# Expert weights read as two neighbouring rows to a partition, in a two-layer diffusion block on one core

## The chip, the cores and the metric

The kernel runs on one core of a Trainium2 chip. The metric is device time in microseconds of one execution, lower is better. All arithmetic on the chip is in 32-bit floats; the large projections split each operand into a high and a low part and take three products.

## The reference, cut to what matters

256 latent tokens and 256 context tokens of width 1024 go through two layers. A layer has four token mixers (a gated delta rule and three attentions), a gated merge of their outputs, an output projection with a first layer norm, and an expert-choice feed-forward with a second norm. The change is about the feed-forward and what feeds it:

```python
def expert_choice_ffn(h, w_router, w_gate, w_up, w_down):
    aff = jax.nn.softmax(jnp.einsum('bnd,de->bne', h, w_router), axis=-1)
    gval, idx = lax.top_k(jnp.swapaxes(aff, 1, 2), cap)        # cap = 32 tokens for each of 16 experts
    xg = jax.vmap(lambda hb, ib: hb[ib])(h, idx)
    a = jnp.einsum('becd,edf->becf', xg, w_gate)
    u = jnp.einsum('becd,edf->becf', xg, w_up)
    y = jnp.einsum('becf,efd->becd', jax.nn.silu(a) * u, w_down)
    ...
```

Each expert has three 1024 x 1024 weight matrices, 12 MB of float32. With 16 experts and two layers that is 384 MB, read once. A sum over d or f may be taken in any order, as long as the rows of the weights and the entries of the tokens are paired alike.

## The kernel before, in words

Work is written in program order and a scheduler of the language orders it on each engine; waits are semaphores. All weight loads are issued by SyncE (SP), one after another in one queue: an SP instruction that waits holds back all loads behind it.

**Streams of weights.** `wload` (L123) loads 1 MB into a tile "w" of 128 partitions x 2048 numbers. `split` and `hilo` (L130, L145) cut a projection's weights into a high part "wh" (copied by ACT) and a low part "wl" (subtracted by DVE or POOL); each part is a tile of 128 x 1024 of its own, three buffers deep (`parts`, L141).

**Merge** (`merge`, L1128). For each of the four branches, in the order 0, 3, 2, 1, the branch's transposed output is loaded from DRAM into "oT" (written oTm), split into "oh" (ACT) and "ol" (DVE), each with one buffer, and multiplied by the branch's weights, split into "bh" and "bl": 8 groups of 6 products (ps_br). Between these groups stand the products of the gates (ps_gate, 24 to a group). Gates of some branches were computed before and come back from DRAM as "thm".

**Output projection, router, experts.** `out_project` (L1164) ends with the first norm and `route`, which transposes the rows of the residual "xz" (ps_xT, L1284) for the router. `moe` then gathers the chosen tokens with one-hot products (ps_xg, L1413; "xgT" holds the result, the contraction on the partitions), four experts at a time, and works through 16 experts: 4 pieces of w_gate_e, 4 of w_up_e (ps_gu, L1458), a transposition of the activated values "eac" (ps_aT, L1475), 4 pieces of w_down_e (ps_dn, L1489). A piece is 256 rows of a weight matrix, 1 MB. `wl` (L1324) gives each piece a slot in turn: 1 MB tiles "w", or pairs of 512 KB tiles "we" that other stages have left (wh with wl, bh with bl, oT with oh), 13 slots in layer 0. Partition p of a piece holds row p and row p + 128: two runs of 4 KB. A pair of tiles takes two DMAs.

```python
# L1327
rows = src[l, e, kk * 256:(kk + 1) * 256, :].rearrange("(k p) f -> p k f", p=P)
# L1340, a pair of tiles
for k, (pool, tag, n) in enumerate(slot):
    w = pool.tile([P, 1024], F32, tag=tag, name="we", bufs=n)
    nc.sync.dma_start(w, rows[:, k])
```

**Modulation** (`mod`, L220): the six vectors of each token stream that scale and shift the norms are a product with w_mod; its pieces are loaded as [128, 2048], 8 KB to a partition. At the start every second piece goes through two tiles "wm" of 512 KB.

## Time and profile before

| | |
|---|---|
| median of 3 runs | 2174.92 us (2173.11, 2174.92, 2190.13) |
| span of the profiled execution | 2171.3 us |
| bytes moved by DMA in it | 553.92 MB |
| busy: PE, DVE, ACT, POOL | 1849.2, 955.9, 503.8, 350.6 us |
| experts of layer 0, first gathered product to last weight | about 729 to 1219 us |
| experts of layer 1 | about 1702 to 2151 us |

The profile is of one execution, and its time is its span; nothing else of that execution is on record. It lies 3.6 us under the median. PE is TensorE's products, PEld its loads of the stationary operand (beside PE). A queue's share is the time that its packets took, over 16 DMA engines and the stretch; packets overlap a little, so it can pass 100%. "A <- B" in a list of waits means that A sat idle until B was done.

### The profile page before, as it was taken

The page shows a single profiled execution, that of the slowest core. Times are in us where ns is not written, and L with a number is a line of the kernel's source. Part 1 is how long each engine was busy: PE and PEld are TensorE (multiplying, and loading weights), DVE is VectorE, ACT ScalarE, POOL GpSimd, SP SyncE. Part 2 cuts the span into 40 slices and gives each one's busy share as a digit, 9 for nine tenths or more (in the row PEclk, how much of TensorE's full clock was granted, in tenths as well). Part 3 has the DMA queues.
Part 4 walks back from the last instruction along what each step waited for, and adds up shares of the span by engine and source line. Part 5 has one row for each costly group of instructions (what it writes and reads, how often), then busy time and mean ns, then how long its engine had stood idle before and what let it go on. Part 6 is the DMA issues. An engine that isn't in the chain of part 4 may idle for free. (4 is left out here: it accounts for less than half of the span.)

```text
span 2171.3 us, 33547 instructions
## 1 busy us (share of the span) xinstructions
PE 1849.2 (85%) x13730; PEld 1199.7 (55%) x13730; DVE 955.9 (44%) x2126; ACT 503.8 (23%) x1038; POOL 350.6 (16%) x380
## 2 busy tenths in 40 slices
PE   6898899989999899988797898899899886676665
PEld 2676778867788555322222376778889542232221
DVE  3859547773226424221121486977755430110102
ACT  2332116752222111000000332246543100000000
POOL 1151330012532000000000125330264000000000
PEclk9999999998999899999999999999999896777767
DMA  7445413117333589999999655302487899999996
GB/s 290 161 170 194 156 36 108 54 59 260 110 126 137 211 335 350 409 409 409 409 409 409 239 194 182 130 24 96 134 271 265 323 408 409 409 409 409 409 409 274
DMA packets 200181, 553.92 MB, mean 255 GB/s; under 512 B 16222, under 2 KB 83164, under 8 KB 194396
## 3 DMA queue, kind: packets, MB, share of 16 engines
q1 hardware_dynamic: 190960, 538.56, 65.6%
q10 hardware_dynamic: 9068, 13.23, 1.7%
q8 instruction: 108, 1.77, 0.3%
q14 instruction: 45, 0.37, 0.1%
HBM read 541.25 MB, written 10.49 MB: 254 GB/s over the span
## 5 line engine op out<-in xcount | busy, mean ns | idle before, releaser
L1458 PE MATMUL ps_gu<-w,xgT 128*32 128x256 f32 (+1 forms) x1632 | 241.2, 533 | 69.5 <-DMA w<-in_w_gate_e_dram 35.5
L149 POOL TENSOR_TENSOR wl<-w,wh 128x1024 fp32r<-128x1024 f32 x62 | 154.1, 2486 | 884.1 <-DMA w<-in_w_in_dram 504.2
L1458 PE MATMUL ps_gu<-we,xgT 128*32 128x256 f32 (+1 forms) x1440 | 204.1, 512 | 38.8 <-DMA we<-in_w_up_e_dram 24.3
L1458 PEld LDWEIGHTS ps_gu<-w,xgT 128*32 128x32 f32 (+1 forms) x1632 | 78.8, 134 | 212.1 <-issue 83.0
L1500 DVE TENSOR_TENSOR y<-ps_dn,g2r 32x512 f32<-32x512 f32 (+1 forms) x128 | 70.9, 554 | 259.0 <-PE ps_dn L1489 257.5
L311 PE MATMUL ps_gate<-hh,wh 128*128 128x512 f32 (+1 forms) x512 | 179.8, 351 | 0.4 <-ACT wh L148 0.4
L313 PE MATMUL ps_gate<-hh,wl 128*128 128x512 f32 (+1 forms) x512 | 179.5, 351 | 0.0
L312 PE MATMUL ps_gate<-hl,wh 128*128 128x512 f32 (+1 forms) x512 | 179.4, 350 | 0.0
L148 ACT CAST wh<-w 128x1024 fp32r<-128x1024 f32 x124 | 129.6, 1049 | 179.2 <-PE ps_gate L312 77.3
L1458 PEld LDWEIGHTS ps_gu<-we,xgT 128*32 128x32 f32 (+1 forms) x1440 | 63.1, 128 | 167.3 <-DMA we<-in_w_up_e_dram 62.1
L1489 PE MATMUL ps_dn<-w,eaT 128*32 128x256 f32 (+1 forms) x896 | 119.1, 522 | 32.5 <-DMA w<-in_w_down_e_dram 26.8
L1468 ACT ACTIVATE eth<-ps_gu 128x512 f32<-128x512 f32 (+1 forms) x32 | 15.7, 491 | 518.4 <-PE ps_gu L1458 518.4
L311 PE MATMUL ps_n<-wh,hh 128*128 128x256 f32 x400 | 116.7, 292 | 7.3 <-DVE c_v L861 3.1
L312 PE MATMUL ps_n<-wl,hh 128*128 128x256 f32 x400 | 115.8, 290 | 8.2 <-POOL wl L149 8.2
L1471 DVE SCALAR_TENSOR_TENSOR eac<-eth,ps_gu 128x512 f32<-128x512 f32 (+1 forms) x32 | 17.7, 554 | 235.1 <-PE ps_gu L1458 235.1
L149 DVE TENSOR_TENSOR wl<-w,wh 128x1024 fp32r<-128x1024 f32 x62 | 85.9, 1385 | 72.9 <-ACT wh L148 72.6
L313 PE MATMUL ps_n<-wh,hl 128*128 128x256 f32 x400 | 115.9, 290 | 0.0
L1489 PE MATMUL ps_dn<-we,eaT 128*32 128x256 f32 (+1 forms) x640 | 93.4, 512 | 15.6 <-DMA we<-in_w_down_e_dram 11.1
L311 PEld LDWEIGHTS ps_gate<-hh,wh 128*128 128x128 f32 x512 | 99.4, 194 | 11.4 <-ACT wh L148 0.8
L312 PEld LDWEIGHTS ps_gate<-hl,wh 128*128 128x128 f32 x512 | 99.2, 194 | 10.8
L313 PEld LDWEIGHTS ps_gate<-hh,wl 128*128 128x128 f32 x512 | 99.0, 193 | 10.8 <-DVE wl L149 0.2
L1470 DVE SCALAR_TENSOR_TENSOR eth<-eth,ps_gu 128x512 f32<-128x512 f32 (+1 forms) x32 | 17.7, 554 | 193.3 <-ACT eth L1468 193.3
(453 smaller groups left out, 3591.2 us busy)
## 6 DMA issues: line engine op xcount, KB each, us to landing
w<-in_w_gate_e_dram SPq DMA_DIRECT2D x75, 1024.0 KB, 13.2
w<-in_w_down_e_dram SPq DMA_DIRECT2D x72, 1024.0 KB, 12.7
w<-in_w_up_e_dram SPq DMA_DIRECT2D x62, 1024.0 KB, 13.9
we<-in_w_up_e_dram SPq DMA_DIRECT2D x120, 512.0 KB, 13.4
w<-in_w_in_dram SPq DMA_DIRECT2D x54, 1024.0 KB, 5.2
we<-in_w_down_e_dram SPq DMA_DIRECT2D x108, 512.0 KB, 14.0
we<-in_w_gate_e_dram SPq DMA_DIRECT2D x96, 512.0 KB, 13.9
w<-in_w_mod_dram SPq DMA_DIRECT2D x44, 1024.0 KB, 5.0
```

The lines of the kernel that those rows point to most:

```text
L148: nc.scalar.copy(h, w)
L149: (nc.gpsimd if j else nc.vector).tensor_tensor(x, w, h.bitcast(F32), op=OP.subtract)
L311: nc.tensor.matmul(ps, lh[k], rh[k], start=(k == 0), stop=False)
L312: nc.tensor.matmul(ps, lh[k], rl[k], start=False, stop=False)
L313: nc.tensor.matmul(ps, ll[k], rh[k], start=False, stop=(k == nk - 1))
L1458: nc.tensor.matmul(ps[M * q:M * q + M, :NF], xg[e // 4][:, 2 * kk + k, e % 4, :], w[k][:, q * NF:(q + 1) * NF], start=(kk == 0 and k == 0) ...
L1468: nc.scalar.activation(th, pss[0][:, :NF], AF.Tanh, scale=0.5)
L1470: nc.vector.scalar_tensor_tensor(th, th, 1.0, pss[0][:, :NF], op0=OP.add, op1=OP.mult)
L1471: nc.vector.scalar_tensor_tensor(ac, th, 0.5, pss[1][:, :NF], op0=OP.mult, op1=OP.mult)
L1489: nc.tensor.matmul(py[M * q:M * q + M, :NF], av[:, fc % nj, fc // nj, :], w[k][:, q * NF:(q + 1) * NF], start=(fc == 0), stop=(fc == 7))
L1500: nc.vector.tensor_tensor(ys[w][32 * e4:32 * e4 + 32, q * NF:(q + 1) * NF], py[o:o + 32, :NF], g2r[o:o + 32, q * NF:(q + 1) * NF], op=OP.mult)
```

## The change

A piece of an expert's weights still has 256 rows, but partition p now holds the rows 2p and 2p + 1, which lie side by side in DRAM: one run of 8 KB. The two halves of a piece are then the even and the odd rows, so everything that is contracted with them is put in the same order by reading with a step of two numbers (`pairs`): the residual's rows in the gather and in the router's transpositions, the activated values in theirs, the router's weights, and the columns of gain, bias and modulation that are applied to the gathered tokens. For these columns the modulation's vectors 3 and 4 are transposed a second time into "modp", and their biases and the first norm's gain and bias are loaded a second time into "vecp", in runs of two numbers.

The pairs of 512 KB tiles become single tiles: wh and wl are the halves of "whl", bh and bl those of "bhl", oT and oh those of "oth". A slot is then filled by one DMA. In layer 0, one early slot (ol with y1) stays a pair, as do two in layer 1. Some small tiles share buffers between the layers.

```diff
 def parts(self, n):
-        return [self.whs[self.nwh].tile([P, 1024], F32R, tag=g, name=g)[:, :n] for g in ("wh", "wl")]
+        t = self.whs[self.nwh].tile([P, 2, 1024], F32R, tag="whl", name="whl")
+        return [t[:, i, :n] for i in range(2)]
 def mod(self, l, g):
-                w = []
-                for j, tag in enumerate(("wh", "wl")):
-                    w.append(self.whp.tile([P, 1024], F32, tag=tag, name="wm"))
-                    nc.sync.dma_start(w[j], src[:, j * 1024:(j + 1) * 1024])
+                w = self.whp.tile([P, 2, 1024], F32, tag="whl", name="wm")
+                nc.sync.dma_start(w.rearrange("p a b -> p (a b)"), src)
+                w = [w[:, 0], w[:, 1]]
...
+        if g:
+            pt = self.pt.tile([P, 512], F32, tag="t", name="ps_mp")
+            for a in range(2):
+                for j in range(2):
+                    nc.tensor.transpose(pt[:, (2 * a + j) * P:(2 * a + j + 1) * P], self.pairs(rows)[:, a, j], self.c("ident"))
...
+            for w2 in range(2):
+                nc.vector.tensor_tensor(dst[:, :, :, w2], src[:, :, :, w2], bc, op=OP.add)
 def merge(self, l, br, first):
-        oT = self.mg.tile([P, 2, 512], F32, tag="oT", name="oTm", bufs=1)
+        oth = self.mg.tile([P, 2, 2, 512], F32R, tag="oth", name="oth", bufs=1)
+        oT, oh = oth[:, 0].bitcast(F32), oth[:, 1]
         nc.sync.dma_start(oT[:, :, :n], self.oT[br])
         ol = self.mg.tile([P, 2, 512], F32R, tag="ol", name="ol", bufs=1)
-        oh = self.mg.tile([P, 2, 512], F32R, tag="oh", name="oh", bufs=1)
...
-                bh, bl = (self.mg.tile([P, 2, 512], F32R, tag=x, name=x, bufs=2) for x in ("bh", "bl"))
+                bhl = self.mg.tile([P, 2, 2, 512], F32R, tag="bhl", name="bhl", bufs=2)
+                bh, bl = bhl[:, 0], bhl[:, 1]
+def pairs(x):
+        return x.rearrange("p (a q j) -> p a j q", q=P, j=2)
 def route(self, t, stats):
-                nc.tensor.transpose(ps[j][:, k * P:(k + 1) * P], z[:, kc * P:(kc + 1) * P], self.c("ident"))
+                nc.tensor.transpose(ps[j][:, k * P:(k + 1) * P], self.pairs(z)[:, kc // 2, kc % 2], self.c("ident"))
 def moe(self, l):
-            order = [self.wpb] * self.NW2[l] + [[(mg, "bh", 2), (mg, "bl", 2)]] * 2 + [[(mg, "oT", 1), (mg, "oh", 1)]]
+            order = [self.wpb] * self.NW2[l] + [[(mg, "bhl", 2)]] * 2 + [[(mg, "oth", 1)]]
...
-                rows = src[l, e, kk * 256:(kk + 1) * 256, :].rearrange("(k p) f -> p k f", p=P)
+                rows = src[l, e, kk * 256:(kk + 1) * 256, :].rearrange("(p k) f -> p k f", k=2)
+                flat = src[l, e, kk * 256:(kk + 1) * 256, :].rearrange("(p k) f -> p (k f)", k=2)
...
-                                nc.tensor.matmul(po, self.xz[:, off[w] + i, k * P:(k + 1) * P],
+                                nc.tensor.matmul(po, self.pairs(self.xz[:, off[w] + i])[:, k // 2, k % 2],
...
-                    nc.tensor.transpose(ps[:, j * P:(j + 1) * P], ac[:, j * P:(j + 1) * P], self.c("ident"))
+                    nc.tensor.transpose(ps[:, j * P:(j + 1) * P], self.pairs(ac)[:, j // 2, j % 2], self.c("ident"))
 def run(self):
+                for i, r in enumerate((R_BMOD + 24, R_L1G)):
+                    nc.scalar.dma_start(self.vecp[:, 16 * i:16 * i + 16].rearrange("p (v j) -> p v j", j=2),
+                                        a["vecs"][l, r:r + 16, :].rearrange("r c -> (r c)").rearrange("(v q j) -> q v j", q=P, j=2))
```

On SP, the loads of layer 0's first two experts stood like this before ("w" and "we" are slots, the last number of a row how often it is repeated):

```order
L127 DMA w<-in_w_down_e_dram 128x2x1024
L1343 DMA we<-in_w_down_e_dram 128x1024 x6
L127 DMA w<-in_w_gate_e_dram 128x2x1024 x3
L1343 DMA we<-in_w_gate_e_dram 128x1024 x2
L1343 DMA we<-in_w_up_e_dram 128x1024 x4
L127 DMA w<-in_w_up_e_dram 128x2x1024 x2
```

And so they stand now:

```order
L127 DMA w<-in_w_down_e_dram 128x2048
L1358 DMA we<-in_w_down_e_dram 128x2048 x3
L127 DMA w<-in_w_gate_e_dram 128x2048 x3
L1358 DMA we<-in_w_gate_e_dram 128x2048
L1358 DMA we<-in_w_up_e_dram 128x2048 x2
L127 DMA w<-in_w_up_e_dram 128x2048 x2
```

The pieces and their order are the same; six DMAs of 512 KB have become three of 1 MB, and every row of 1024 numbers has become one of 2048.

On SP in the merge of layer 0, before. The middle number in oT_0, thd_3_1 and so on is the branch (for thd with its column group behind); oTm is the load of a branch's output, thm that of its gates:

```order
L826 DMA oT_3_203<-ot 128x1024
L1133 DMA oTm<-oT_3_203 128x1024
...
L1150 DMA thm<-thd_0_6_4741 128x512
L1150 DMA thm<-thd_0_7_4770 128x512
L127 DMA w<-in_w_gate_e_dram 128x2x1024
L1150 DMA thm<-thd_3_0_4809 128x512
L1150 DMA thm<-thd_3_1_4838 128x512
L1133 DMA oTm<-oT_2_202 128x1024
L127 DMA w<-in_w_in_dram 128x8x256
```

The same place now:

```order
L1163 DMA thm<-thd_0_6_4721 128x512
L1163 DMA thm<-thd_0_7_4750 128x512
L1146 DMA oth<-oT_3_195 128x1024
L127 DMA w<-in_w_gate_e_dram 128x2048
...
L1163 DMA thm<-thd_3_6_4985 128x512
L1163 DMA thm<-thd_3_7_5014 128x512
L1146 DMA oth<-oT_2_194 128x1024
L127 DMA w<-in_w_in_dram 128x8x256
```

The load of branch 3's output has moved from right behind that branch's store to behind the last gates of branch 0, and that of branch 2 from behind the second gates of branch 3 to behind its last ones: each now follows the branch before it.

## Rows read from the trace of the kernel before

**Rows 1.** Page, part 2, the span in 40 slices: DMA busy tenths, GB/s.

```profile
DMA  7445413117333589999999655302487899999996
GB/s 290 161 170 194 156 36 108 54 59 260 110 126 137 211 335 350 409 409 409 409 409 409 239 194 182 130 24 96 134 271 265 323 408 409 409 409 409 409 409 274
```

**Rows 2.** Busy time by stretch: PE, PEld, DVE, ACT, POOL, clock, DMA share, GB/s.

```profile
740.00:850.00 110.00, 110.00 (x630) 60.17 (x630) 34.58 (x70) 17.37 (x36) 0.00 (x0) 1.00 0.84 323
840.00:850.00 10.00, 10.00 (x59) 5.00 (x60) 9.36 (x16) 0.38 (x1) 0.00 (x0) 1.00 0.55 189
868.00:1194.00 326.00, 281.00 (x1171) 84.94 (x1171) 66.02 (x108) 13.99 (x24) 0.00 (x0) 0.99 1.03 409
1210.00:1220.00 10.00, 10.00 (x40) 3.00 (x42) 0.46 (x2) 1.65 (x4) 0.00 (x0) 1.00 1.02 336
1700.00:1710.00 10.00, 10.00 (x83) 7.20 (x84) 3.07 (x12) 2.42 (x5) 0.00 (x0) 0.82 0.33 110
1720.00:1730.00 10.00, 10.00 (x163) 7.58 (x155) 2.53 (x7) 1.29 (x3) 0.00 (x0) 1.00 1.03 412
1750.00:2140.00 390.00, 266.00 (x2599) 99.59 (x2597) 50.29 (x114) 14.10 (x35) 0.00 (x0) 0.74 1.03 409
```

**Rows 3.** Waits of SP's queue from 868 to 1194 us: total, times, longest.

```profile
SPq L127 <- DMA w<-in_w_up_e_dram: 32.5, 16, 2.2
```

**Rows 4.** DMA by queue from 868 to 1194 us: packets, MB, share of 16 engines.

```profile
q1 hardware_dynamic: 35505, 133.26, 102.5%
```

**Rows 5.** The same from 34 to 38 us, when only w_in moves (1 KB runs).

```profile
DMA packets 1384, 1.39 MB, mean 348 GB/s; under 512 B 25, under 2 KB 1384, under 8 KB 1384
```

**Rows 6.** The same from 9.5 to 12 us (w_mod, mostly 8 KB runs).

```profile
DMA packets 185, 1.07 MB, mean 429 GB/s; under 512 B 16, under 2 KB 16, under 8 KB 92
```

**Rows 7.** The same from 17.5 to 22 us (q1 w_mod, q10 4 KB rows).

```profile
q1 hardware_dynamic: 179, 1.16, 62.1%
q10 hardware_dynamic: 182, 0.74, 41.1%
```

**Rows 8.** The same from 1264 to 1274.2 us, two single loads of w_mod.

```profile
q1 hardware_dynamic: 288, 2.10, 60.7%
```

**Rows 9.** Tile oTm from 500 to 660 us (layer 0): ns min/median/max, landing.

```profile
L148 ACT CAST oh<-oTm x3: 1039/1043/1055, 520.4 to 599.2; 128x1024 fp32r<-128x1024 f32 x3
L149 DVE TENSOR_TENSOR ol<-oTm,oh x3: 2550/2582/3427, 521.5 to 600.3; 128x1024 fp32r<-128x1024 f32 x3
...
DMA to landing us min/median/max: 3.6/3.6/3.6
```

**Rows 10.** Tile oTm from 1570 to 1660 us (layer 1).

```profile
L148 ACT CAST oh<-oTm x3: 609/611/614, 1581.0 to 1628.3; 128x512 fp32r<-128x512 f32 x3
L149 DVE TENSOR_TENSOR ol<-oTm,oh x3: 945/2270/2772, 1581.6 to 1629.0; 128x512 fp32r<-128x512 f32 x3
...
DMA to landing us min/median/max: 3.2/3.2/3.2
```

**Rows 11.** Busy time in one stretch of each merge, columns as in rows 2.

```profile
610.00:620.00 10.00, 10.00 (x45) 8.05 (x44) 2.33 (x3) 2.15 (x3) 2.94 (x2) 1.00 0.32 105
1640.00:1650.00 10.00, 10.00 (x86) 10.00 (x85) 3.04 (x4) 4.42 (x6) 4.52 (x4) 1.00 0.83 269
```

**Rows 12.** Waits of PE, 500 to 660 us, then 1570 to 1660 us.

```profile
PE ps_br L312 <- DVE ol L149: 3.4, 2, 2.9
PE ps_br L311 <- ACT oh L148: 1.9, 1, 1.9
...
PE ps_br L312 <- DVE ol L149: 2.2, 2, 1.7
...
PE ps_br L311 <- ACT oh L148: 1.6, 1, 1.6
```

**Rows 13.** Tile ps_xg, whole span.

```profile
L1413 PEld LDWEIGHTS ps_xg<-OH,xz x384: 186/192/338, 729.1 to 1755.7; 128*128 128x128 f32 x192
```

**Rows 14.** DMA view, issues: KB each, us to landing.

```profile
wr<-in_w_router_dram ACTq DMA_DIRECT2D x2, 64.0 KB, 3.4
```

More of the change, by code (lines that the diff above doesn't have):

```diff
@@ L1194, in out_project @@
         self.last_stats = stats[3]
+    @staticmethod
+    def pairs(x):
+        return x.rearrange("p (a q j) -> p a j q", q=P, j=2)
     def xt(self, t):
@@ L1332, in wl @@
                 if not isinstance(slot, list):
-                    w = self.wload(rows, (2, 1024), pool=slot)
-                    return [w[:, k] for k in range(2)]
+                    w = self.wload(flat.unsqueeze(1), (1, 2048), pool=slot)
+                    return [w[:, 0, k * 1024:(k + 1) * 1024] for k in range(2)]
                 if len(slot) == 1:
                     pool, tag, n = slot[0]
-                    w = pool.tile([P, 2, 1024], F32, tag=tag, name="we", bufs=n)
-                    nc.sync.dma_start(w, rows)
-                    return [w[:, k] for k in range(2)]
+                    w = pool.tile([P, 2048], F32, tag=tag, name="we", bufs=n)
+                    nc.sync.dma_start(w, flat)
+                    return [w[:, k * 1024:(k + 1) * 1024] for k in range(2)]
                 out = []
@@ L1552, in run @@
         self.all_of(self.mod(0, 0))
-        s1 = self.keep.tile([P, 8, 2], F32, name="s1")
+        s1 = self.keep.tile([P, 8, 2], F32, tag="s1", name="s1", bufs=1)
         nc.vector.tensor_scalar_add(s1, self.modc[0][:, 8:16, :], 1.0)
@@ L1579, in run @@
                 st["m"] = self.pool(f"ai{l}", stack=sa, side="right")
+                self.vecp = self.keep.tile([P, 32], F32, tag="vecp", name="vecp", bufs=1)
+                self.modp = self.keep.tile([P, 2, 8, 2], F32, tag="modp", name="modp", bufs=1)
+                for i, r in enumerate((R_BMOD + 24, R_L1G)):
+                    nc.scalar.dma_start(self.vecp[:, 16 * i:16 * i + 16].rearrange("p (v j) -> p v j", j=2),
+                                        a["vecs"][l, r:r + 16, :].rearrange("r c -> (r c)").rearrange("(v q j) -> q v j", q=P, j=2))
                 with ExitStack() as sx:
@@ L1657, in run @@
                     self.final_rows(0)
-            v = self.vec[l]
-            s2_ = self.keep.tile([P, 8, 2], F32, name=f"s2{l}")
-            nc.vector.tensor_scalar_add(s2_, self.modc[l][:, 32:40, :], 1.0)
+            s2_ = self.keep.tile([P, 8, 2], F32, tag="s2", name=f"s2{l}", bufs=1)
+            nc.vector.tensor_scalar_add(s2_, self.modp[:, 1], 1.0)
             ws = [0, 1] if l == 0 else [0]
-            self.c2 = {w: self.comb(f"c2_{l}{w}", v[:, R_L1G:R_L1G + 8], v[:, R_L1B:R_L1B + 8], s2_[:, :, w], self.mcol(l, 3, w)) for w in ws}
+            vp = self.vecp
+            self.c2 = {w: self.comb(f"c2_{l}{w}", vp[:, 16:24], vp[:, 24:32], s2_[:, :, w], self.modp[:, 0, :, w], f"c2_{w}") for w in ws}
             self.g1r = {}
@@ L1677, in run @@
                 v = self.vec[0]
-                s1b = self.keep.tile([P, 8, 2], F32, name="s1b")
+                s1b = self.keep.tile([P, 8, 2], F32, tag="s1", name="s1b", bufs=1)
                 nc.vector.tensor_scalar_add(s1b, self.modc[1][:, 8:16, :], 1.0)
```

21 lines of the change are left out of this document (13 added, 8 removed).

## The prediction

> **What bounds the kernel now.** I read the page's line of slices first, then busy time by stretch, then the DMA view of single stretches, and last the waits and tiles of the merge. In the slices [rows 1] two plateaus stand out: the DMA engines are busy without a gap and move 409 GB/s, in layer 0's experts and in layer 1's. The stretches [rows 2] show the same in detail. From 868 to 1194 us the DMA share is 1.03 while PE is busy for 281 of 326 us, and from 1750 to 2140 us it is 1.03 while PE is busy for 266 of 390: there the weights' transfers set the pace and PE follows. Ahead of each plateau it is the other way round. From 740 to 850 us PE is busy for all 110 us, and the last 10 of them have the DMA at 0.55; from 1700 to 1710 us it is at 0.33: loads wait for slots that PE has yet to empty. On the plateau SP waits for an earlier transfer to land [rows 3], not for PE. So I count as bound by transfers 850 to 1215 us (in the row from 1210 the rate falls to 336 GB/s) and 1720 to 2140 us: 365 + 420 = 785 us.
>
> Work outside these stretches delays the end one for one, because a plateau begins when PE reaches it.
>
> **The change part by part.**
>
> *Longer runs.* The bytes stay. What can change is the time per byte. On the plateau 133.26 MB took 102.5% of 16 engines for 326 us, 5346 us of engine time, 24.9 bytes per ns in packets of 4 KB [rows 4]. Packets of 8 KB exist in this trace, in w_mod, and there are three ways to price them. First, two short stretches at the start, where the engines are full. In one the mean is 429 GB/s [rows 6]; 93 of its 185 packets are of 8 KB and carry 0.76 of its 1.07 MB. In the other, q1, with 1.16 MB in 179 packets, 6.5 KB each in the mean, moved them in 62.1% of 16 x 4.5 us, 25.9 bytes per ns, while q10's 4 KB rows beside it made 25.0 [rows 7]. That is 4.9% and, against its own neighbour, 3.6% more for runs that are only partly long. Both stretches are so short that one packet per engine more or less moves them by two per cent or more. Second, a fixed cost per packet: with 1 KB runs the rate is 348 GB/s [rows 5], with 4 KB 409. If a packet costs as much as its bytes plus f, then 409/348 = 4 x (1024 + f) / (4096 + f), f = 254 bytes, and 8 KB packets run at 2 x 4350 / 8446 = 1.030 of the rate. Third, single loads with nothing beside them: 2.10 MB in 60.7% of 16 x 10.2 us, 21.2 bytes per ns [rows 8], 15% slower than the plateau; these include the start of each load, which a full queue hides, so I keep it only as the far end. I take 3.3%, near the fixed cost and under the mixed stretches: 785 x (1 - 1/1.033) = 25 us less. The far ends are 4.9% (-37 us) and 21.2 bytes per ns (+137 us).
>
> The Trainium skill has a rule that would give less. "DMA: Bandwidth & Descriptors", section "Why small descriptors are slow (HBM only)", puts the fixed cost at about 3 beats of 32 bytes a packet; by it 8 KB gains 1.2% over 4 KB, and the sum would have 9 us here instead of 25. The trace does not agree: by that rule 1 KB would cost 7% against 4 KB, and the two rates above differ by 17.5%.
>
> PE has room for 25 us less: in layer 0, 11 of them fall into a stretch in which PE idles for 45 of 326 us.
>
> *Full slots.* Where two DMAs filled a slot, one does. The waits behind a slot's second half become waits for the whole, half a piece (1.3 us at 409 GB/s) later for what only needed the first; a full queue hides this except at the last piece of a layer. I put 1 us for both layers.
>
> *Merge: oT and oh in one buffer.* This is the part that costs. Before, the next branch's output could be loaded while the present one was multiplied, since oT is free once it is split. Now the load waits until the last product that reads oh, and so the transfer's latency joins the chain from branch to branch; the order on SP shows it, each load behind its predecessor's last gates. What queues behind the waiting load are w_in, w_br and gates for later groups and spare expert pieces. The chain in layer 0: landing 3.6, cast 1.04, subtraction 2.58 = 7.2 us [rows 9]; in layer 1: 3.2 + 0.61 + 2.27 = 6.1 us [rows 10]. Cover is one group of 24 gate products, at 10 us for 45 of them in layer 0 and for 86 in layer 1 [rows 11]: 5.3 and 2.8 us. Bare are 1.9 and 3.3 us for each of three transitions, 15.6 us in all. The kernel already pays some: PE waited 3.4 + 1.9 us and 2.2 + 1.6 us for oh and ol [rows 12], 9.1 us. That leaves 6.5 us; I add 1.5 because one of the three covers is shorter than a full group, and take 8 us. Ends: -2 us if the scheduler finds other gates for every gap, +16 us if none of the old waits is saved.
>
> *Added work.* Four loads of "vecp" in runs of 8 bytes; the nearest load is w_router's, 64 KB in 64-byte runs, landed after 3.4 us [rows 14]. Two of them stand ahead of the first small projection's weights on ACT's queue; I put 1 us at the start, between 0 and 7. The transpositions and additions for modp are 16 and 8 small instructions in stretches full of projections: 1 us. The start's "wm" in full tiles gives a few tenths back.
>
> *Reading with a step of two.* No stationary operand in this trace is read so, so the price has no row. The near one is the gather's: a load of 128 x 128 takes 192 ns [rows 13]. I take nothing, and keep a doubling as the far end, below. "SBUF — State Buffer" of the Trainium skill, section "Door 1: The DMA port swizzle (why `[64,N]` ≈ `[32,N]`)", says reads run at full speed while two of them fall into a line of 16 bytes, which a step of two numbers keeps; by it the far end is nothing, and no run here shows it yet.
>
> Sum: -25 + 1 + 8 + 2 = -14 us. The profiled span of 2171.3 us becomes 2157; it lies 3.6 us under the median of 2174.92, so I predict **2161 us** for a median.
>
> **The rivals.** *The merge's cover holds.* PE finds gates for all gaps and the merge costs 0 to 2 us: 2175 - 25 + 4 = 2154 or less, 2151 with the upper rate. For it speaks that the order on PE was moved with the loads (more gates ahead of the first product of a branch); against it that in layer 1 a group covers only 2.8 of 6.1 us.
>
> *Long runs give little.* If what separates 348 from 409 GB/s is not a cost per packet but where 1 KB runs lie in DRAM, the plateau stays near 409. Then the costs remain: 2175 + 11 = 2186 with no gain, 2177 with a third of it. The skill's rule above belongs here. Against it stand the two mixed stretches.
>
> *The stepped reads are dear: slower than before.* The gather's 384 loads stand in stretches that PE sets (740 to 850 us, PE busy for 110 of 110; 1700 to 1756 us). If each takes twice its 192 ns, that is 74 us: 2161 + 74 = 2235. It decides against the change from 14 us / 384 = 36 ns more on each load.
>
> **How the numbers follow.** The forecast has a chance of 0.50, alone from 2150 to 2172; the merge's cover 0.24; little gain 0.17; dear reads 0.09. A measurement of this kernel can tell about 1% from no change, 21.7 us: faster means under 2153. Faster takes 0.16 of the forecast and 0.18 of the cover's 0.24: 0.34. Slower takes 0.07 of the dear reads, 0.02 of little gain and 0.01 of the rest: 0.10. The range, 2143 to 2184, reaches to the upper rate with full cover and to no gain at all, and leaves the dear reads out.
>
> **What would show it.** In the profile after: a plateau near 422 GB/s instead of 409, packets of the expert loads halved in number and together some 3% shorter; PE waiting for oh or ol in rows of 2 to 4 us at the branch changes, about 17 us instead of 9; the gather's loads still at 192 ns; PE's pace from 740 to 850 us unchanged. A plateau at 409, a merge that is longer by over 16 us, or gather loads above 230 ns would make the forecast wrong.

## The result, and the profile after

The changed kernel is slower. Its median is 2194.01 us in 20 runs (2179.36 to 2210.82), that of the kernel before 2179.97 in 20 runs beside it (2170.39 to 2195.23); the ratio is 1.0056, 95% interval 1.0036 to 1.0075. A second series on another chip gave 1.0050 (1.0021 to 1.0078). The forecast of 2161 us (2143 to 2184) is missed, and in direction: 14 us less were expected, 12 us more came.

The transfers did what was foretold. The page's slices after, to be read against [rows 1]:

```profile
DMA  7445513106433588999999655402377799999996
GB/s 279 161 160 193 163 43 112 49 35 223 157 106 126 183 310 347 421 421 421 421 421 422 234 175 187 139 24 89 109 250 255 289 420 421 421 420 421 421 420 256
```

The plateaus are at 421 GB/s instead of 409. The stretches that answer to [rows 2], the last of them shifted by the 18 us that the gather starts later:

```profile
868.00:1194.00 326.00, 288.70 (x1226) 91.86 (x1224) 68.15 (x117) 15.56 (x27) 0.00 (x0) 1.00 1.01 421
1750.00:2140.00 390.00, 269.11 (x2856) 117.32 (x2848) 55.15 (x127) 19.14 (x47) 0.00 (x0) 0.79 1.01 421
...
758.00:868.00 110.00, 110.00 (x627) 61.74 (x628) 34.19 (x69) 17.19 (x36) 0.00 (x0) 1.00 0.82 318
```

The DMA view of 868 to 1194 us, to [rows 4]: 18800 packets where 35505 were, 7.3 KB each in the mean, and 136.93 MB moved instead of 133.26.

```profile
q1 hardware_dynamic: 18800, 136.93, 101.0%
```

The gather's loads of the stationary operand, now read with a step of two, to [rows 13]:

```profile
L1433 PEld LDWEIGHTS ps_xg<-OH,xz x384: 192/196/336, 747.2 to 1782.9; 128*128 128x128 f32 x192
```

196 ns instead of 192: the step of two is almost free, as "SBUF — State Buffer" of the Trainium skill, section "Door 1: The DMA port swizzle (why `[64,N]` ≈ `[32,N]`)", has it. The gather of layer 0 takes 111 us in both profiles, and PE is busy without a gap in it.

So the time is lost elsewhere. I took the first and last product of every PSUM tile (the names ps_...) in both profiles and followed how late the changed kernel is. The spans differ by 2188.6 - 2171.3 = 17.3 us:

| where | the delay grows by |
|---|---|
| layer 0, start to the last preparation of the merge (ps_wrb) | +12.2 us |
| layer 0, merge and output projection, to ps_xT | +5.6 us |
| layer 0, experts, from the first ps_xg to the last ps_dn | -10.0 us |
| layer 1, ps_ab to the last attention output (ps_ot) | +10.1 us |
| layer 1, merge and output projection, to ps_xT | +7.1 us |
| layer 1, experts | -11.4 us |
| small rest between these, and the end | +3.7 us |

**The clock ahead of the merges.** The first and fourth row are the surprise, because no new wait stands in them. I cut both profiles at the same work (the first ps_ab, ps_gc, last ps_kk, first ps_gate, ps_stk and ps_wrb). The kernel before by stretch, columns as in [rows 2]:

```profile
0.00:41.20 41.20, 22.71 (x106) 8.27 (x106) 8.97 (x29) 8.32 (x18) 2.41 (x7) 0.96 0.97 356
41.20:126.40 85.20, 77.83 (x418) 52.29 (x418) 58.54 (x101) 32.78 (x53) 23.04 (x32) 0.92 0.45 152
126.40:158.20 31.80, 30.04 (x334) 24.54 (x334) 20.51 (x43) 4.98 (x9) 17.30 (x59) 0.99 0.46 159
158.20:256.60 98.40, 88.67 (x751) 75.00 (x751) 71.01 (x136) 26.28 (x43) 24.65 (x24) 0.99 0.56 192
256.60:344.50 87.90, 79.55 (x953) 61.77 (x950) 46.30 (x98) 19.06 (x34) 27.17 (x30) 0.94 0.21 71
344.50:508.70 164.20, 153.61 (x965) 129.47 (x963) 118.31 (x361) 103.70 (x294) 14.80 (x6) 0.97 0.24 85
```

The changed kernel, the same work:

```profile
0.00:44.20 44.20, 21.87 (x106) 8.48 (x106) 9.10 (x28) 8.19 (x18) 2.39 (x7) 0.87 0.93 333
44.20:128.70 84.50, 77.74 (x419) 52.75 (x419) 58.42 (x101) 32.81 (x53) 23.18 (x31) 0.92 0.46 152
128.70:163.60 34.90, 32.91 (x332) 27.14 (x332) 20.66 (x43) 4.99 (x9) 17.37 (x59) 0.89 0.44 149
163.60:263.40 99.80, 91.50 (x760) 77.96 (x759) 70.27 (x140) 26.34 (x43) 25.48 (x24) 0.97 0.58 189
263.40:355.50 92.10, 84.88 (x965) 66.22 (x962) 46.22 (x99) 19.52 (x35) 27.00 (x30) 0.91 0.22 68
355.50:520.90 165.40, 157.11 (x952) 131.21 (x950) 112.32 (x359) 104.28 (x292) 14.52 (x6) 0.93 0.24 82
```

Read the length, PE's busy time (the number behind it) and the clock (third from the end). PE's idle time, length minus busy, is 56.3 us before and 54.9 after: no wait was added. Busy time lost to the lower clock is busy x (1 - clock); summed over stretches of 2 us, which rounds less than these rows, it is 18.0 us before and 32.0 after. That is +14.0 - 1.4, the whole delay. Two of the falls to the lower clock are new (from 132 and 217 us), and three last longer than before: 10 us instead of 3 (from 23 us), 17 instead of 10 (from 269 us) and 17 instead of 3 (from 463 us). In layer 1, up to the merge, the same sums are 10.5 and 24.2 us lost, and idle 32.5 and 30.2. As rows, from the first ps_ab to the last ps_ot, before and then changed:

```profile
1246.50:1562.00 315.50, 282.96 (x2705) 243.22 (x2703) 250.40 (x557) 133.60 (x297) 99.87 (x140) 0.96 0.36 122
```

```profile
1255.00:1580.60 325.60, 295.34 (x2712) 252.49 (x2710) 248.41 (x561) 133.63 (x297) 99.08 (x140) 0.92 0.36 117
```

What such a fall looks like: after a short idle, the changed kernel's rows of 6 us at 126 and 132 us,

```profile
126.00:132.00 6.00, 4.10 (x33) 2.76 (x31) 5.96 (x4) 0.41 (x1) 3.08 (x4) 1.00 0.78 258
...
132.00:138.00 6.00, 5.51 (x31) 4.99 (x32) 2.09 (x9) 1.04 (x5) 1.44 (x9) 0.51 0.23 97
```

and the kernel before in the same place:

```profile
126.00:132.00 6.00, 3.91 (x37) 3.63 (x37) 4.47 (x7) 0.37 (x1) 2.60 (x3) 1.00 0.86 322
132.00:138.00 6.00, 5.95 (x72) 4.27 (x73) 3.01 (x9) 1.53 (x5) 4.82 (x27) 1.00 0.01 3
```

Both idle for 2 us in the first 6 (PE waits for DVE there). Then one goes on at 2.4 GHz (clock 1.00), the other falls to 1.2 GHz (0.50). The counts of products, 72 and 31, are not of quite the same work, which comes 2.4 us later in the changed kernel; for the same work, the third row of each table above, it takes 34.9 us instead of 31.8. "TensorE: Matmul & The Clock Gate" of the Trainium skill, section "HAM oscillation — how this bites in real kernels", describes a kernel in which waits of PE send it back to the low clock each time. The fall after idle time agrees with it; that nearly the same idle time is followed by a fall in one kernel and by none in the other is not told there.

**The waits in the merges.** PE's waits in the changed kernel's layer 0, to [rows 12]:

```profile
PE ps_gate L323 <- ACT thm L1161: 3.6, 1, 3.6
PE ps_br L323 <- ACT oth L149: 2.9, 1, 2.9
PE ps_gate L323 <- ACT whl L149: 2.1, 1, 2.1
PE ps_gate L325 <- DVE whl L150: 1.2, 1, 1.2
```

and in layer 1:

```profile
PE ps_br L323 <- ACT oth L149: 4.5, 2, 2.5
PE ps_br L323 <- DVE thm L1173: 3.9, 3, 1.9
...
PE ps_gate L323 <- ACT thm L1161: 0.5, 1, 0.5
```

The kernel before waits for 5.9 and 5.8 us in the two merges (9.1 of these 11.7 are [rows 12]), the changed one for 10.5 and 10.2: 9.0 us more. What SP waits for ahead of the load of a branch's output has changed as the prediction has it, from the subtraction that frees oT to the products that read oh. Before, layer 0:

```profile
SPq L1133 <- DVE ol L149: 2.5, 1, 2.5
```

The changed kernel, layer 0 and layer 1:

```profile
SPq L1146 <- PE ps_br L325: 1.7, 1, 1.7
...
SPq L1146 <- PE ps_br L325: 2.9, 1, 2.9
```

The chain behind that load is there, in the tile's own rows of layer 1: a load that lands after 3.2 us, a cast of 0.62 and a subtraction of 0.88 us, three times.

```profile
L149 ACT CAST oth<-oth x3: 619/619/621, 1602.4 to 1655.8; 128x512 fp32r<-128x512 f32 x3
L150 DVE TENSOR_TENSOR ol<-oth x3: 727/876/1212, 1603.0 to 1656.5; 128x512 fp32r<-128x512 f32 x3
...
DMA to landing us min/median/max: 3.2/3.2/3.2
```

### The profile page after: what moved, and what is told of

It is laid out like the page before. It is cut to its first block, busy times and chain, and to the rows that moved or that the text cites. A ratio compares the mean times of both kernels' runs of the same rounds, so it can differ in the third digit from the quotient of the medians.

```text
span 2188.6 us, 33257 instructions
## 1 busy us (share of the span) xinstructions
PE 1864.7 (85%) x13746; PEld 1234.8 (56%) x13746; DVE 941.8 (43%) x2134; ACT 504.8 (23%) x1038; POOL 350.1 (16%) x380
## 5 line engine op out<-in xcount | busy, mean ns | idle before, releaser
L150 POOL TENSOR_TENSOR whl<-w,whl 128x1024 fp32r<-128x1024 f32 x62 | 153.8, 2480 | 874.7 <-ACT whl L149 780.2
L1478 PE MATMUL ps_gu<-w,xgT 128*32 128x256 f32 (+1 forms) x1632 | 233.0, 512 | 48.4 <-DMA w<-in_w_up_e_dram 25.4
L323 PE MATMUL ps_gate<-hh,whl 128*128 128x512 f32 (+1 forms) x512 | 182.9, 357 | 6.2 <-ACT thm L1161 4.1
L325 PE MATMUL ps_gate<-hh,whl 128*128 128x512 f32 (+1 forms) x512 | 182.0, 356 | 1.7 <-DVE whl L150 1.2
L324 PE MATMUL ps_gate<-hl,whl 128*128 128x512 f32 (+1 forms) x512 | 181.5, 355 | 0.0
L149 ACT CAST whl<-w 128x1024 fp32r<-128x1024 f32 x124 | 129.5, 1047 | 149.9 <-PE ps_gate L325 54.1
L324 PE MATMUL ps_n<-whl,hh 128*128 128x256 f32 x400 | 118.3, 296 | 6.7 <-POOL whl L150 6.7
L323 PE MATMUL ps_n<-whl,hh 128*128 128x256 f32 x400 | 118.6, 296 | 6.2 <-DVE c_v L873 2.4
L325 PE MATMUL ps_n<-whl,hl 128*128 128x256 f32 x400 | 118.0, 295 | 0.0
L323 PEld LDWEIGHTS ps_gate<-hh,whl 128*128 128x128 f32 x512 | 101.3, 198 | 18.1 <-ACT thm L1161 4.8
L325 PEld LDWEIGHTS ps_gate<-hh,whl 128*128 128x128 f32 x512 | 101.3, 198 | 13.8 <-DVE whl L150 1.8
L324 PEld LDWEIGHTS ps_gate<-hl,whl 128*128 128x128 f32 x512 | 101.2, 198 | 10.5
L150 DVE TENSOR_TENSOR whl<-w,whl 128x1024 fp32r<-128x1024 f32 x62 | 84.9, 1370 | 39.6 <-ACT whl L149 39.4
```

Of the source, the lines that this page charges most:

```text
L149: nc.scalar.copy(h, w)
L150: (nc.gpsimd if j else nc.vector).tensor_tensor(x, w, h.bitcast(F32), op=OP.subtract)
L323: nc.tensor.matmul(ps, lh[k], rh[k], start=(k == 0), stop=False)
L324: nc.tensor.matmul(ps, lh[k], rl[k], start=False, stop=False)
L325: nc.tensor.matmul(ps, ll[k], rh[k], start=False, stop=(k == nk - 1))
L1478: nc.tensor.matmul(ps[M * q:M * q + M, :NF], xg[e // 4][:, 2 * kk + k, e % 4, :], w[k][:, q * NF:(q + 1) * NF], start=(kk == 0 and k == 0) ...
```

## The experiments

Each run is timed against the kernel before on the same chip. The last column is the mean granted clock over the span, averaged over all timed runs of the kernel.

| kernel | median us (runs) | ratio, 95% interval | clock |
|---|---|---|---|
| before, four series | 2181.9 (120) | | 0.920 |
| changed, again (e6) | 2196.23 (12) | 1.0050 (1.0021 to 1.0078) | 0.907 |
| e1 oT and oh apart | 2172.03 (12) | 0.9958 (0.9935 to 0.998) | 0.915 |
| e2 wh and wl apart | 2186.13 (12) | 1.0028 (1.0004 to 1.0051) | 0.918 |
| e3 no added work | 2176.4 (11) | 0.998 (0.9961 to 1.0) | 0.916 |
| e4 all pairs apart | 2178.41 (12) | 0.9987 (0.997 to 1.0003) | 0.921 |
| e5 before, again | 2184.68 (8) | 1.0004 (0.9969 to 1.0039) | 0.917 |
| e7 oh and ol in one tile, oT alone | 2171.96 (10) | 0.9952 (0.992 to 0.9984) | 0.912 |
| e8 e7, vector columns by transposes | 2176.57 (12) | 0.9956 (0.9925 to 0.9986) | 0.911 |
| e9 before, later start | 2183.3 (12) | 1.0012 (0.9989 to 1.0034) | 0.920 |
| e10 before, small loads | 2198.61 (6) | 1.0091 (1.0068 to 1.0114) | 0.916 |
| e11 8 KB runs alone | 2174.17 (12) | 0.9968 (0.9946 to 0.9989) | 0.922 |
| e12 changed, later start | 2195.6 (12) | 1.0054 (1.0028 to 1.0079) | 0.909 |
| e13 before, wh and wl in one tile | 2185.34 (12) | 1.0013 (1.0 to 1.0027) | 0.915 |
| e14 e7 without the added work | 2163.32 (6) | 0.9915 (0.9892 to 0.9937) | 0.917 |
| e15 changed, vector columns by transposes | 2195.16 (6) | 1.0055 (1.0033 to 1.0077) | 0.907 |
| e16 changed, small loads but no modp | 2175.37 (12) | 0.9973 (0.9952 to 0.9993) | 0.915 |

**First four: which part costs.** e1:

```diff
-        oth = self.mg.tile([P, 2, 2, 512], F32R, tag="oth", name="oth", bufs=1)
-        oT, oh = oth[:, 0].bitcast(F32), oth[:, 1]
+        oT = self.mg.tile([P, 2, 512], F32, tag="oT", name="oTm", bufs=1)
...
+        oh = self.mg.tile([P, 2, 512], F32R, tag="oh", name="oh", bufs=1)
```

> The changed kernel, but oT and oh are two tiles again (and serve a weight piece in two 4 KB halves, one piece in ten or so). Theory A: the merges' extra 13 us (+5.6 in layer 0, +7.7 in layer 1, from the first instruction of the first branch to the last of the fourth) come from the next branch's load of oT, which in the shared buffer waits for the last matmul on oh: apart, the merges take 141.5 and 95 us again, PE's waits at the branch changes fall back to about 9 us, the time falls by 11 to 13 us, to about 1.000 of the kernel before, while the delays ahead of the merges (+11 to +12 us in layer 0, +10 in layer 1) stay. Rival B: the merges' loss comes from the pair bh and bl in one tile, or from a lower granted clock there: then the time moves by under 3 us (ratio 1.004 to 1.007).

Measured: 0.9958, some 21 us below the changed kernel by the ratios and more than expected. Up to the merge of layer 0 the two profiles agree within 0.2 us until the attention at 475 us; then PE waits for 6.0 us instead of 10.5 in that merge, and for 4.6 instead of 10.2 in layer 1's. Theory A holds, and the merge's price is larger than its waits: busy time lost to the clock in the two merges is 4.3 us where the changed kernel has 14.2 (and the kernel before 10). Its two merges as stretches:

```profile
523.00:705.20 182.20, 172.98 (x888) 145.17 (x888) 68.25 (x89) 45.80 (x56) 76.94 (x39) 0.99 0.46 154
1570.30:1689.90 119.60, 114.55 (x931) 112.76 (x930) 64.41 (x85) 47.06 (x71) 64.70 (x40) 0.98 0.79 271
```

The same work (from the last ps_wrb or ps_ot to ps_xT) takes 192.8 and 128.6 us in the changed kernel, 187.3 and 121.5 before.

e2 goes back to the two tiles wh and wl (and two wm) in the same way:

```diff
-        t = self.whs[self.nwh].tile([P, 2, 1024], F32R, tag="whl", name="whl")
-        return [t[:, i, :n] for i in range(2)]
+        return [self.whs[self.nwh].tile([P, 1024], F32R, tag=g, name=g)[:, :n] for g in ("wh", "wl")]
```

> The changed kernel, but wh and wl (and the first modulation piece's wm in them) are two tiles each again, and three or four pieces in ten are loaded in two 4 KB halves with 4 KB runs. Theory A: the shared tile makes the cast to its high half wait for the last matmul that reads either half, and this delays the early stages: +12 us up to the merge of layer 0 and +10 in layer 1 go, less some 7 us of the plateau's gain (a third of the expert bytes back at 409 GB/s): ratio about 0.998. Rival B: the early delays come from the added loads of the vector columns and from the added transposes: then only the start (wm) may move by 1 to 3 us, and the ratio gets worse, 1.006 to 1.010.

1.0028, between both. The plateau stays at 419 GB/s, so less is lost by halves than expected. The early delay of layer 0 up to ps_stk is still there (10 us): so far theory A is not borne out. Behind it, it is, in this profile: layer 0's attention, from ps_stk to ps_wrb, loses 3.4 us to the clock where the changed kernel loses 10.4, and layer 1 up to its merge takes 316 us, as before.

e3 leaves out the block `if g:` in mod (transposes and additions) and the loads of vecp, and reads the old columns:

```diff
-            nc.vector.tensor_scalar_add(s2_, self.modp[:, 1], 1.0)
+            nc.vector.tensor_scalar_add(s2_, self.modc[l][:, 32:40, :], 1.0)
...
-                for i, r in enumerate((R_BMOD + 24, R_L1G)):
-                    nc.scalar.dma_start(self.vecp[:, 16 * i:16 * i + 16].rearrange("p (v j) -> p v j", j=2),
...
```

> The changed kernel without the added work: no loads of the vector columns in pair order (vecp) and no second set of transposes and additions (modp); the router's and gather's scale and shift columns are taken in the old order, so the numbers that come out are not the reference's. Theory A: 2048 packets of 8 bytes ahead of the first layer's weights, and the transposes behind them, cause the early delays: without them the +3 us at the first projection, the +11 to +12 ahead of the merge of layer 0 and the +10 of layer 1 go, ratio about 0.996. Rival B: full tiles cause them (the shared whl): the time falls by 2 to 4 us only, the bare price of the added work, ratio 1.003 to 1.005.

0.998: 15 to 17 us below the changed kernel, more than rival B's size and less than theory A's. Yet layer 0's early delay is 9 of 11 us with the added work gone; what went is 5 us in the merge of layer 0 and 9 us in layer 1 ahead of its merge.

e4 is the edits of e1 and e2 and, for bh and bl:

```diff
-                bhl = self.mg.tile([P, 2, 2, 512], F32R, tag="bhl", name="bhl", bufs=2)
-                bh, bl = bhl[:, 0], bhl[:, 1]
+                bh, bl = (self.mg.tile([P, 2, 512], F32R, tag=x, name=x, bufs=2) for x in ("bh", "bl"))
```

> The changed kernel with all three pairs apart (wh and wl, bh and bl, oT and oh), so that only the 8 KB runs in the other slots, the reordered contraction and the added work are left. If the shared tiles cause both the merges' loss (13 us) and the early delays (20 us), and about half of the pieces lose the 8 KB runs (10 us of the gain of 22), the ratio is about 0.995. If the early delays belong to the added work, it is 1.003 to 1.005, with the merges at their old 141.5 and 95 us. If the merges stay long, their loss is not the tiles' at all.

0.9987, the merges back at their old length within 1 us (their loss is the tiles'), and the plateau at 416 GB/s.

**Next four: is it the profile, and a better version.** e5 and e6 are the two kernels unchanged.

> The kernel before, unchanged, for a second profile. The first one has a span of 2171.3 us, 8 us under the median of its runs. Theory A: its lead ahead of layer 0's merge (9 to 11 us against the changed kernel, and 7 to 10 against three variants that share little but the 8 KB runs) is mostly this one execution's granted clock: a second profile reaches the first attention instructions of layer 0 (ps_stk, 344.5 us in the first) 5 us or more later, and has a span near 2179. Rival B: the lead is the program's, as the changed kernel and its variant with oT and oh apart agree within 0.2 us up to that point: then it is at 344 to 346 us again, and the change costs 9 us ahead of the merge in a way not yet found.

> The changed kernel, unchanged, beside the other kernels of this series, and a second profile. Ratio 1.004 to 1.008; PE waits and milestones as in its first profile within 2 us up to the end of layer 0's merge. If its stages wander by 5 us and more between two profiles, stage differences of that size between single profiles say nothing.

The second profile of before has ps_stk at 346.0 us: rival B for layer 0, its early lead is the program's. In layer 1 the same profile is 5.9 us later ahead of the merge, with the busy time lost to the clock at 16.1 instead of 10.5 us, so half of the 10 us there is one execution's luck. And the first profile, a span of 2171.3 us, was a short one: the median over 120 runs is 2181.9. The second profile of the changed kernel is 3 us later from 156 us on (one more fall) and otherwise the same up to layer 0's merge. Between the two second profiles the rows of the table of delays are +15.2, +4.2, -7.8, +3.5, +6.8 and -10.5 us: the same signs, with less in layer 1 ahead of its merge.

e7 makes the full tile from two parts that live equally long:

```diff
-        oth = self.mg.tile([P, 2, 2, 512], F32R, tag="oth", name="oth", bufs=1)
-        oT, oh = oth[:, 0].bitcast(F32), oth[:, 1]
+        oT = self.mg.tile([P, 2, 512], F32, tag="oT", name="oTm", bufs=1)
...
+        ohl = self.mg.tile([P, 2, 2, 512], F32R, tag="ohl", name="ohl", bufs=1)
+        oh, ol = ohl[:, 0], ohl[:, 1]
```

> The changed kernel, but the full tile is made of oh and ol (both are written by the cast and the subtraction and read by the same matmuls), and oT has a 4 KB tile of its own, so that its load waits only for the subtraction of the branch before. Theory A: the merges' loss was oT sharing a buffer with oh: the merges become as short as with all tiles apart (layer 0 within 3 us of 137 us, layer 1 of 92), and the pieces in this slot keep 8 KB runs: ratio 0.994 to 0.997. Rival B: any full tile in the merge costs, because the cast to oh now also waits for the last reader of ol: merges 5 us longer than with oT and oh apart, ratio 0.998 to 1.001.

0.9952, theory A: all slots full, the plateau at 421 GB/s, the merges at 183.7 and 119.1 us. This version beats both kernels. PE's waits in its layer 1:

```profile
PE ps_gate L323 <- ACT thm L1161: 1.9, 1, 1.9
PE ps_br L324 <- DVE ohl L150: 1.3, 1, 1.3
PE ps_br L323 <- DVE thm L1173: 1.2, 3, 0.4
```

The wait for the cast of a branch's output (ACT oth) no longer stands in them.

e8 is e7 with other loads for the vector columns (vr is a tile of 16 x 256, pv one of PSUM):

```diff
-                    nc.scalar.dma_start(self.vecp[:, 16 * i:16 * i + 16].rearrange("p (v j) -> p v j", j=2),
...
+                    nc.scalar.dma_start(vr[8 * i:8 * i + 8], a["vecs"][l, r:r + 16, :].rearrange("(v h) c -> v (h c)", h=2))
...
+                    nc.tensor.transpose(pv[:, 16 * j:16 * j + 16], vr.rearrange("v (q j) -> v j q", j=2)[:, j], self.c("ident")[:16, :16])
```

> As the variant with oh and ol in one tile, and the vector columns in pair order come from two loads of 8 rows of 1 KB and two transposes on PE (16 rows of 256 values, every other column) in place of two loads of 2048 packets of 8 bytes. Theory A: those packets are 3 us of the delay at the first projection and make layer 1's start late: ratio 0.002 to 0.004 below the variant with oh and ol in one tile. Rival B: the price of the added work is in the second set of transposes and additions (modp) and the packets run beside other work: ratio the same within 0.001.

0.9956: rival B, the small packets cost nothing that can be measured. Its start is 0.8 us earlier, no more.

**Next four: what makes the clock fall.** e9 adds a copy of 512 KB within DRAM ahead of the activations' load:

```diff
+        scr = self.drp.tile([P, 1024], F32, name="scr")
+        nc.scalar.dma_start(scr, a["x"].rearrange("o (t p) d -> p (o t) d", p=P)[:, 0])
         self.load_x(0, x2d)
```

> The kernel before with one more transfer: 512 KB of x copied within DRAM, issued ahead of the activations' load; nothing reads the copy, and the order on PE is the same row for row. Theory A: the changed kernel's lag ahead of the merges is lost at TensorE's lower clock (14 us more of it than in the kernel before up to layer 0's merge, with PE's idle time and its work at full clock equal within 1.5 us), and whether a short idle stretch is followed by a fall depends on when it comes: then a start some 2 us later is enough to change the loss at the lower clock (18 and 21 us up to layer 0's merge in two profiles of before) to 25 us or more, with falls after 126 to 132 us where before has none, and the time rises by more than the start's delay. Rival B: the falls belong to the changed tiles and loads themselves: the loss at the lower clock stays at 18 to 21 us, and the time rises by the start's 1 to 3 us only, ratio 1.000 to 1.002.

In its profile the shift has theory A's effect: 25.1 us are lost to the clock up to layer 0's merge, and a fall stands where before had none,

```profile
132.00:138.00 6.00, 5.57 (x41) 5.11 (x42) 1.94 (x9) 1.40 (x5) 2.72 (x17) 0.77 0.23 97
138.00:144.00 6.00, 6.00 (x46) 3.35 (x45) 1.93 (x4) 0.84 (x1) 5.36 (x31) 0.50 0.10 16
```

but over its 12 runs neither the time (1.0012) nor the mean clock (0.920) moves beyond the start's delay. A shift moves falls about; this one, 1.3 us at the first ps_ab, doesn't make the kernel slow. As a cause of the 12 us my theory fell.

e10 adds the changed kernel's two loads of vecp to the kernel before, into a scratch tile in DRAM:

```diff
+                vecp = self.drp.tile([P, 32], F32, name=f"vecp{l}")
```

> The kernel before with the two loads of the vector columns in pair order alone, in each layer where the changed kernel has them (2048 packets of 8 bytes each; they go to a scratch place in DRAM that nothing reads). The bare price of the packets, as in the changed kernel: the first projection (ps_ab) 1 to 3 us later in layer 0. Theory A (the clock by the timing): loss at the lower clock up to layer 0's merge 25 us or more, ratio 1.002 to 1.005. Rival B: 1 to 3 us and no more, ratio 1.000 to 1.002, falls as in before.

1.0091, but this run answers another question than it asked: with nothing to wait for, all four loads were issued at the start, and ps_ab began 15 us late. These were 4096 packets of 8 bytes. PE waited 13.0 us for pieces of w_mod in that profile, and 1.5 us in the kernel before:

```profile
PE ps_mod L237 <- DMA wm<-in_w_mod_dram: 13.0, 3, 10.4
```

The changed kernel has no such wait. At the start it has 2048 of these packets, they come later, and they go into a tile; which of the three matters was not tested.

e11 is the edits of e3 and e4 together.

> The 8 KB runs alone: all three pairs of tiles apart as in the kernel before, none of the added loads, transposes and additions (the router's and gather's scale and shift columns in the old order, so the numbers that come out are not the reference's); contraction reordered, and the order on PE that of the kernel before row for row. About half of the pieces keep 8 KB runs: -10 us in the plateaus as with all pairs apart. Theory A: without a shift in time the early stages run as in before: layer 0's merge begins within 2 us of 508.7, layer 1's within 7 us of it, ratio 0.994 to 0.997. Rival B: what slowed the early stages in every variant is the part all of them share (runs, reorder): merge of layer 0 at 516 us or later, ratio 0.998 to 1.001.

0.9968, as theory A has it by the time, though in its profile layer 0's merge begins at 514.7 us, between both. The mean clock is the highest of all, 0.922; 416 GB/s on the plateau.

e12 is e9's edit on the changed kernel.

> The changed kernel with the same extra transfer of 512 KB ahead of the activations' load. Theory A: the loss at the lower clock up to layer 0's merge (32 and 36 us in two profiles) and in layer 1 ahead of its merge (22 and 19 us) moves by 4 us or more in one of them, up or down, though no tile, wait or order of the change is undone. Rival B: both stay within 2 us of the changed kernel's, and the time rises by the start's 1 to 3 us.

1.0054 and a mean clock of 0.909, as the changed kernel: rival B by the time; in the profile 29.6 us are lost up to layer 0's merge. With e9, this speaks for a low clock that belongs to the program and not to when it starts, as far as one shift can tell.

**Last four: which part of it.** e13 puts e2's edit the other way round on the kernel before.

> The kernel before, with wh and wl (and the first modulation's wm in them) in one tile each, as in the changed kernel, and nothing else of the change: 4 KB runs everywhere, oT and oh apart. Theory A: the shared tile lowers the granted clock, since the cast to the high half waits for the last matmul on either half and the work then comes in other pieces: mean clock over the runs 0.916 or less (before 0.920 over 97 runs), time 5 to 15 us up, ratio 1.002 to 1.007. Rival B: the shared tile does nothing by itself: clock 0.919 to 0.921, ratio 0.998 to 1.001.

The mean clock is as low as theory A has it (0.915); the time rises by less (1.0013). In its profile layer 0's merge begins at 517.9 us, 9 us later than in both profiles of before, with no part of the change in it but this tile (e9 has 517.1 with the tiles apart, so one profile does not prove it). In layer 0's attention 9 us are lost to the clock against 4.3 to 4.8 in both profiles of before,

```profile
354.00:517.90 163.90, 155.56 (x953) 130.25 (x951) 112.41 (x359) 104.31 (x292) 14.57 (x6) 0.94 0.24 85
```

and layer 0's merge is 3.7 us shorter, which gives most of that back.

All 18 profiles agree on that attention. The seven with wh and wl apart (before, e2, e4, e5, e9, e10, e11) lose 3.4 to 5.0 us to the clock in it, the eleven with them in one tile 8.8 to 10.8, with 8 to 11 us of idle time in the first group and 8 to 9 in the second. The one tile also puts PE's work there in another order: the gates' products stand at other places among the attention's, alike in all eleven, while the seven have the order of the kernel before. Whether the order or the waits on the shared tile bring the lower clock was not separated.

e14 is the edits of e7 and e3 together.

> The variant with oh and ol in one tile, without the added loads, transposes and additions (scale and shift columns in the old order, so the numbers that come out are not the reference's). If the price of the added work is the 17 us that the changed kernel shows without it, and adds to the 22 of the shared oT and oh: ratio 0.987 to 0.989. If it is the 5 us seen with all pairs apart: 0.992 to 0.994. If it is nothing once oT is apart: 0.995 to 0.996.

0.9915, 8 us below e7: nearest to the middle one of the three sizes.

e15 is e8's edit of the loads on the changed kernel, e16 is e3 with the loads kept.

> The changed kernel with the vector columns in pair order made from two loads of 8 rows of 1 KB and two transposes, in place of 2048 packets of 8 bytes twice; oT and oh in one buffer as in the changed kernel. If the small packets are what the added work costs: ratio 0.998 to 1.001. If not: 1.003 to 1.006.

> The changed kernel with the small loads but without the second set of transposes and additions (modp); the scale and shift columns are taken in the old order, so the numbers that come out are not the reference's. If the transposes and additions are what the added work costs: ratio 0.998 to 1.001. If the loads: 1.003 to 1.006.

1.0055 and 0.9973: it is the transposes and additions. They are these few instructions in the changed kernel, 16 x 0.283 us on PE, 8 x 0.158 on DVE:

```profile
L257 PE MATMUL ps_mp<-const,mrow x16: 279/283/286, 179.4 to 1398.7; 128*128 128x128 f32 x16
L263 DVE TENSOR_TENSOR modp<-ps_mp,vecp x8: 153/158/167, 183.2 to 1401.6; 128x8 f32<-128x8 f32 x8
```

5.8 us of work; leaving it out gave 17 to 18 us, though the rest of PE's work stands in the same order in both. The spans of the two profiles differ by 17.2 us, and 15.5 of them are busy time lost to the clock: 2.9 ahead of layer 0's merge, 3.2 in it, 9.4 in layer 1 ahead of its merge. Layer 1's scan, from ps_stk to ps_ot, is the plainest place. The changed kernel, then e16:

```profile
1429.50:1496.90 67.40, 62.65 (x793) 53.54 (x790) 47.15 (x123) 25.03 (x67) 18.71 (x24) 0.82 0.06 19
```

```profile
1416.60:1478.90 62.30, 57.06 (x792) 49.07 (x789) 47.11 (x123) 24.81 (x67) 18.68 (x24) 0.92 0.07 21
```

The same products, the transposes 28 us past, 0.82 against 0.92. But e1, e6, e7, e9 and e12 have 0.82 too, e15 has 0.69, and e2, e4 and e8 have 0.92 with modp in them, so this place alone doesn't decide. Over the whole way from ps_ab to the last ps_ot in layer 1, the seven profiles with modp and with wh and wl in one tile take 323.0 to 335.2 us, but for e8 with 318.2; the eleven that lack one or both take 314.5 to 321.3. So there the loss seems to need both parts; with one profile of most kernels this is likely, not shown.

**The sum of the parts.** Four kernels form a square; ratios as us of 2182:

| | without the added work | with it |
|---|---|---|
| oT apart (e14, e7) | -18.5 | -10.5 |
| oT and oh in one buffer (e3, changed) | -4.4 | +10.9 to +12 |

The shared buffer costs 14 us alone and 21 to 23 with the added work; the added work costs 8 alone and 15 to 17 with the shared buffer. With all pairs apart (e11, e4) it costs 4. Each difference has 6 to 9 us of uncertainty, so that the two cost more together than singly is possible, not shown.

## Why the prediction was wrong

*Longer runs, -25 us, and full slots, +1: right.* 421 GB/s against 422, and -10.0 - 11.4 = -21.4 us in the two expert stages. The fixed cost for each packet gave a factor of 1.030, and 409 x 1.030 is the 421 that came. The half that keeps 8 KB runs in e4 and e11 runs at 416 GB/s, in between. The rivals that long runs give little and that stepped reads are dear are out.

*Merge, +8 us: the waits right, the price too small.* PE waits for 9.0 us more, and merge and output projection take 5.6 + 7.1 = 12.7 us longer than before. The rest of that is busy time lost to the clock: 14.2 us against 10. Against kernels that differ in the shared oT and oh alone the price is 14 to 23 us, as these lose less to the clock (4.3 us in e1) than the kernel before. That PE's added pauses bring the lower clock is likely, not shown. The rival that the cover holds is out too.

*Added work, 1 us for modp's small instructions and 1 for vecp: the step that failed most.* vecp costs 0.8 to 1.9 us at the start (e8, e15 and e16 beside e7, the changed kernel and e3), near its 1 us. modp's 5.8 us of instructions were counted as if hidden beside projections; leaving them out of the changed kernel gave 17 to 18 us (e16). All the added work together costs 8 us with oT apart and 4 with all pairs apart. What was costed was the instructions' own time, not that of the work around them.

*wh and wl in one tile: no term at all.* The sum has the full slots that it makes and the start's "wm", but nothing for the other order on PE that it brings: 8.8 to 10.8 us lost to the clock in layer 0's attention instead of 3.4 to 5.0. Alone (e13) it gives most of this back in the merge.

*What these have in common* is that the sum kept the pace of all PE's other work as one execution had it, as if PE's clock were given. Ahead of the two merges it put 2 us; measured were 12.2 + 10.1 = 22.3 us in the first pair of profiles and 15.2 + 3.5 = 18.7 in the second, with no more idle time of PE. Its busy time lost to the clock grew by 27.7 and by 19 us there, as much or more. The mean clock is 0.920 before and 0.907 to 0.909 after, and within the runs of one kernel 0.001 goes with 1.2 us (before) to 2.0 us (changed). By these slopes the fall of 0.011 to 0.013 goes with 13 to 26 us, the size of what is missing. This is a rough measure, as the mean counts stages in which the clock costs nothing: from 1750 to 2140 us, where transfers set the pace, the clock is 0.74 before [rows 2] and 0.79 in the changed kernel's first profile.

*The base.* "It lies 3.6 us under the median" and "its time is its span" are not quite so: where both are on record a run's time is 1.7 to 2.2 us longer than its span, so the profiled execution took some 2173 us. By 120 runs that is 9 us under the median, not 3.6. A forecast of 14 us under 2181.9 would have been 2168, which changes nothing in its sign.

What stays open is why the clock falls more often. PE's idle time ahead of the merges doesn't grow, and one later start changes nothing in the mean. The shared tile wh and wl (e13), the shared oT and oh (e1), and modp (e16) each lower it; by which pauses, or by which order of the work, was not found.

## What to carry to other kernels

Don't put a part that a prefetch lands in (oT) in one tile with a part that is read to the end (oh): it joins the next load to the end of the present products. Two parts that are written and read together are safer, but look at what the scheduler makes of them: oh with ol cost nothing that can be measured (e7 against e1), wh with wl changed the order on PE and its clock. Where PE sets the pace, small added instructions and pauses can cost up to three times their duration (17 to 18 us for 5.8 in e16): compare the mean granted clock of both kernels over many runs, and split each stage into idle time and busy x (1 - clock) before looking for a wait. One profile is one draw; here it was 9 us from its median, nearly as much as the effect sought.

## What the runs showed of the hardware

- The mean granted clock differs from program to program (0.907 to 0.922 over 16 kernels with nearly the same work) and is a draw in single executions: 20 runs of the changed kernel went from 0.902 to 0.915, and from 2211 to 2179 us with it.
- The fall after an idle stretch of 2 us near 130 us stands in both profiles of the changed kernel (clock 0.51 and 0.50 from 132 to 138 us) and in e1's (0.51), and in neither of the kernel before (1.00 twice), which idles there for 2.1 and 1.7 us of 6 (the others for 1.9 to 2.1); with its start 1.3 us later (e9) the kernel before falls too.
- With 4096 packets of 8 bytes to DRAM at the start (e10) the first ps_ab came 15 us later; the changed kernel's 2048 into a tile cost under 2 us (e16 against e3). Number, place and time of the packets differ, so this does not say which matters.
- A stationary operand read with a step of two 32-bit numbers loads in 196 ns against 192.
